# Where two of eight activation slots lie in SBUF: one slot shifted instead of two

## The chip, the core and the metric

The kernel runs on one core of a Trainium2 chip. The metric is the device time of one execution in microseconds; less is better. A profile of one execution gives the start and duration of every instruction on each engine. PE is TensorE's stream of matmuls, PEld its weight loads, DVE is VectorE, ACT is ScalarE, POOL is GpSimd, SP the queue that issues most DMAs.

## What is computed

The reference is one step of a two-layer diffusion trunk on 128 context tokens and 128 latent tokens of width 2048, all in fp32. Cut to what matters here:

```
for l in range(2):
    shift, scale, gate = adaLN(c) @ ada_w[l]
    h = rms_norm(x) * (1 + scale) + shift
    x = x + gate * mixer_l(h)            # attention | conv, or S5 | attention, with in and out projections
    h = rms_norm(x) * (1 + scale2) + shift2
    a = relu(h @ mlp_w1[l])              # 2048 -> 8192
    x = x + gate2 * ((a * a) @ mlp_w2[l])  # 8192 -> 2048
```

Nearly all the work is projections of a [256, K] activation by a large weight matrix. The two MLPs are the largest part.

## The kernel before

**Tiling.** Activations are kept transposed: a tile has 128 features on the partitions and the 256 tokens along the free axis. An output tile of 128 features is summed in one PSUM bank over all input tiles. `part` (L525) does eight input tiles (K = 1024) of one output tile; `linear` (L542) calls it twice. Most parts have eight blocks; a few have four.

**Split precision.** Weights and activations are both split into a high and a low fp32r half. A weight piece of 128x1024 arrives by DMA in `raw`, ACT writes its rounded half `wh`, DVE writes the rest `wl`. An activation tile becomes a slot of 512 elements: 256 of the high half, then 256 of the low half; ACT writes the first, DVE the second (`put`, L609). `block` (L518) is the inner step, three matmuls of 256 columns for one input tile: wh by the high half, wh by the low half, wl by the high half. Every matmul has a weight load of its own. The trace shows a block as two rows: `lin<-hl,wh` x2, then `lin<-hl,wl` x1. A block's length is the time from its `wh` row to the next block's `wh` row.

**Where activations lie.** The class `Arena` (L78) is one SBUF tile named `hl` with three groups. A group holds eight slots, for input tiles k with k % 8 = 0 to 7, so a part of eight blocks walks through the slots 0 to 7 of one group. In the built program the arena begins 384 bytes past a multiple of 512 and slots are 2048 bytes apart; all groups keep that remainder. So an unshifted slot lies at 384 past a multiple of 512 bytes, for the high and the low half alike. `SHIFT` adds elements of 4 bytes to the start of a slot. The weights `wh` and `wl` lie at 64 past a multiple of 512 throughout. Some activations, half or all of an MLP chunk's hidden tiles, lie in a pool of their own, also named `hl` in the trace: there all slots lie at 384, with no shift. Those for the not yet normalised input of an MLP or layer (`wide`, 258 columns) are packed differently and are not touched by `SHIFT`.

**Counts.** All projections come to 5632 blocks (16,896 matmuls). 304 of them are wide, 1152 read the pool, and the other 4176 read shiftable slots, 522 for each of the slots 0 to 7.

**Order.** A recorder plays all strands of the program against a cost table and writes down one fixed order for each engine. `part` lets other strands in between blocks before k = 2, 4 and 6 (`BREAKS`, L158): matmuls of attention, of S5, or of the adaLN projection (`ada`, L635) then stand between two blocks of a part.

Of the kernel before, what the change touches and what calls it, by code (L numbers as in the profile page):

```python
# [77 lines left out]
class Arena:  # L78
# [2 lines left out]

    SLOT, GROUP, WIDE, SHIFT = 512, 8 * 512 + 128, 516, (0, 0, 0, 0, 0, 0, 32, 40)

    def __init__(self, kern, pool):
        self.kern, self.n = kern, 0
# [1903 lines left out]
```

## Time and profile before

| | us |
|---|---|
| median of 3 runs (2397.22 to 2399.66) | 2398.15 |
| the profiled execution | 2397.81 |
| its span, first to last instruction | 2396.0 |
| PE busy | 2307.9 |
| DVE busy | 1695.7 |
| ACT busy | 1153.0 |

A matmul's row has its start and a modelled duration of about 0.28 us, of which the next matmuls overlap the larger part; what a matmul costs the stream is the distance from its start to the next start, about 0.113 us. So the distances between rows are to be read, not the durations. The rows give starts to 10 ns; a difference of a few ns shows when several blocks are added up.

### The profile page before, as it was taken

What the parts mean: (1) busy time and instruction counts of PE and PEld (TensorE: products, weight loads), DVE (VectorE), ACT (ScalarE), POOL (GpSimd) and SP (SyncE); (2) the same over time, 40 slices, a digit from 0 to 9 for tenths busy, and PEclk for the clock granted to TensorE, in tenths of its full rate; (3) what the DMA queues carried; (4) which work ended last, traced back from release to release, by engine and by line L of the source; (5) the groups of instructions that cost most, each with busy time, mean ns of one, the idle gap of its engine ahead of it and who ended that gap; (6) DMA issues with size and microseconds to landing.
All of it is one profiled execution on the core that took longest, in us unless ns stands there. A gap on an engine that the chain in (4) does not pass through costs nothing.

```text
span 2396.0 us, 49506 instructions
## 1 busy us (share of the span) xinstructions
PE 2307.9 (96%) x20152; PEld 2107.8 (88%) x20152; DVE 1695.7 (71%) x2957; ACT 1153.0 (48%) x1894; POOL 173.1 (7%) x293
## 2 busy tenths in 40 slices
PE   6999999999999999999999978899999999999997
PEld 1788887888999999999999757699999999999997
DVE  1489985677889898888767534566999855655565
ACT  1364457466444434434455744445744333543553
POOL 0000000000011011101000246000000000000000
PEclk9999999999999999999999988899999999999998
DMA  9979997879678889879877877766588855555552
GB/s 384 334 265 317 326 315 260 297 263 326 217 253 308 309 313 304 309 272 340 280 240 252 291 287 258 259 231 203 170 292 290 276 195 192 192 193 190 193 188 95
DMA packets 179637, 627.64 MB, mean 262 GB/s; under 512 B 21376, under 2 KB 21392, under 8 KB 179152
## 3 DMA queue, kind: packets, MB, share of 16 engines
q1 hardware_dynamic: 169920, 595.67, 71.6%
q0 software_dynamic: 9488, 28.81, 3.9%
q8 instruction: 158, 2.59, 0.4%
q14 instruction: 71, 0.58, 0.1%
HBM read 602.17 MB, written 26.41 MB: 262 GB/s over the span
## 4 chain that ended last, share of the span: by engine, by line
PE 85%; DMA 4%; DVE 4%; ACT 3%; POOL 3%; issue 1%; DVEq 0%; SPq 0%; ACTq 0%; POOLq 0%
PE lin L60 75%; PE ada L60 5%; POOL rt L60 2%; DMA raw<-in_ada_w 1%; DVE wl L60 1%; ACT wh L60 1%; DMA raw<-in_ew_in 1%; POOL hs L60 1%; DMA raw<-m3d 1%; PE m1T L60 1%; PE po L60 1%; ACT hs L60 0%; PE ps L60 0%; DVE hl L60 0%; DMA raw<-in_w 0%
## 5 line engine op out<-in xcount | busy, mean ns | idle before, releaser
L60 PE MATMUL lin<-hl,wh 128*128 128x256 f32 (+1 forms) x11200 | 1981.8, 281 | 5.5 <-ACT wh L60 5.0
L60 PEld LDWEIGHTS lin<-hl,wh 128*128 128x128 f32 x11200 | 1703.1, 189 | 97.4 <-issue 60.4
L60 PE MATMUL lin<-hl,wl 128*128 128x256 f32 (+1 forms) x5600 | 1559.4, 278 | 12.1 <-DVE wl L60 11.9
L60 PEld LDWEIGHTS lin<-hl,wl 128*128 128x128 f32 x5600 | 1055.6, 189 | 14.7 <-DVE wl L60 14.7
L60 DVE TENSOR_TENSOR wl<-raw,wh 128x1024 fp32r<-128x1024 f32 (+1 forms) x716 | 857.6, 1207 | 272.0 <-ACT wh L60 268.7
L60 ACT CAST wh<-raw 128x1024 fp32r<-128x1024 f32 (+1 forms) x716 | 738.6, 1036 | 507.6 <-PE lin L60 260.4
L60 PE MATMUL ada<-raw,condp 128*32 128x512 f32 (+1 forms) x1408 | 188.9, 574 | 20.1 <-DMA raw<-in_ada_w 19.9
L60 DVE SCALAR_TENSOR_TENSOR x<-lin,mod,x 128x128 f32<-128x128 f32 x320 | 97.1, 345 | 92.5 <-PE lin L60 92.4
L60 DVE SCALAR_TENSOR_TENSOR va<-raw,condp,va 128x1024 f32<-128x1024 f32 x120 | 148.4, 1278 | 0.0
L60 ACT ACTIVATE ms<-lin 128x256 f32<-128x256 f32 x114 | 43.6, 383 | 136.1 <-PE lin L60 136.0
L60 ACT CAST hl<-mq 128x256 fp32r<-128x256 f32 x128 | 51.9, 406 | 109.9 <-DVE mq L60 109.8
L60 PEld LDWEIGHTS ada<-raw,condp 128*32 128x32 f32 x1408 | 33.1, 109 | 74.9 <-DMA raw<-in_ada_w 34.1
L60 DVE SCALAR_TENSOR_TENSOR cv<-cin,pke,cv 128x256 f32<-128x256 f32 x232 | 96.6, 477 | 0.0
L60 ACT ACTIVATE sq<-x 128x256 f32<-128x256 f32 x75 | 31.0, 417 | 116.4 <-DVE x L60 114.5
L60 DVE SCALAR_TENSOR_TENSOR mq<-lin,ms 128x256 f32<-128x256 f32 x114 | 47.9, 421 | 53.3 <-ACT ms L60 53.2
L60 DVE TENSOR_TENSOR hl<-mq,hl 128x256 fp32r<-128x256 f32 x128 | 53.6, 421 | 27.4 <-ACT hl L60 27.4
L60 POOL TENSOR_TENSOR x<-x,rb 128x512 f32<-128x512 f32 (+1 forms) x2 | 4.2, 2130 | 906.0 <-ACT rb L60 906.0
L60 DVE TENSOR_TENSOR acc<-acc,sq 128x256 f32<-128x256 f32 x75 | 31.8, 423 | 32.3 <-ACT sq L60 30.5
L60 DVE TENSOR_TENSOR hl<-h,hl 128x256 fp32r<-128x256 f32 (+1 forms) x112 | 45.3, 419 | 9.1 <-ACT hl L60 8.7
L60 ACT CAST hl<-h 128x256 fp32r<-128x256 f32 (+1 forms) x112 | 42.7, 401 | 12.1 <-DVE h L60 11.4
L60 POOL DMA_DIRECT2D m3d<-m x32 | 21.5, 677 | 342.8 <-DVE m L60 341.6
L60 DVE TENSOR_TENSOR w<-s5z,bc 128x576 f32<-128x576 f32 x64 | 45.5, 752 | 0.6
(281 smaller groups left out, 1167.8 us busy)
## 6 DMA issues: line engine op xcount, KB each, us to landing
raw<-in_w SPq DMA_DIRECT2D x512, 512.0 KB, 5.1
raw<-in_ada_w SPq DMA_DIRECT2D x352, 512.0 KB, 6.2
raw<-in_ew_in SPq DMA_DIRECT2D x68, 512.0 KB, 6.1
raw<-in_ow_in SPq DMA_DIRECT2D x40, 512.0 KB, 6.2
raw<-in_ada_w SPq DMA_DIRECT2D x64, 256.0 KB, 6.2
raw<-in_ew_out SPq DMA_DIRECT2D x32, 512.0 KB, 5.9
raw<-in_ow_out SPq DMA_DIRECT2D x32, 512.0 KB, 4.5
m3d<-m POOLq DMA_DIRECT2D x32, 256.0 KB, 6.6
```

The costliest lines, as they stand in the source:

```text
L60: return f(out, *a, **kw)
```

## The change

`SHIFT` has one entry for each slot of a group. Before, slot 6 is moved by 32 elements (128 bytes, to 0 past a multiple of 512) and slot 7 by 40 (160 bytes, to 32 past). After, slot 6 is not moved (384 past) and slot 7 is moved by 32 (0 past).

```
-    SLOT, GROUP, WIDE, SHIFT = 512, 8 * 512 + 128, 516, (0, 0, 0, 0, 0, 0, 32, 40)
+    SLOT, GROUP, WIDE, SHIFT = 512, 8 * 512 + 128, 516, (0, 0, 0, 0, 0, 0, 0, 32)
```

Nothing else differs: the size of the arena is the same, every engine has the same instructions in the same order, and they wait for the same semaphores.

## Rows read from the trace of the kernel before

**Rows 1.** The page: parts 1 and 4, and two groups of part 5.
```profile
PE 2307.9 (96%) x20152; PEld 2107.8 (88%) x20152; DVE 1695.7 (71%) x2957; ACT 1153.0 (48%) x1894; POOL 173.1 (7%) x293
...
PE 85%; DMA 4%; DVE 4%; ACT 3%; POOL 3%; issue 1%; DVEq 0%; SPq 0%; ACTq 0%; POOLq 0%
...
L60 PE MATMUL lin<-hl,wh 128*128 128x256 f32 (+1 forms) x11200 | 1981.8, 281 | 5.5 <-ACT wh L60 5.0
...
L60 PE MATMUL lin<-hl,wl 128*128 128x256 f32 (+1 forms) x5600 | 1559.4, 278 | 12.1 <-DVE wl L60 11.9
```

**Rows 2.** Stages: length, busy us of PE, PEld, DVE, ACT, POOL; granted clock, DMA.
```profile
300.00:450.00 150.00, 145.17 (x1164) 119.44 (x1162) 101.10 (x218) 91.22 (x193) 5.94 (x11) 0.98 0.86 294
...
600.00:750.00 150.00, 150.00 (x1425) 145.44 (x1424) 133.30 (x232) 63.78 (x92) 22.05 (x35) 1.00 0.75 252
...
1350.00:1500.00 150.00, 122.64 (x1274) 99.96 (x1266) 59.71 (x108) 73.76 (x124) 77.69 (x134) 0.90 0.79 283
...
2100.00:2250.00 150.00, 150.00 (x1315) 150.00 (x1314) 85.94 (x110) 65.77 (x79) 0.00 (x0) 1.00 0.58 194
```

**Rows 3.** Timeline of PE near the end: start us, us, instruction.
```profile
2371.45 0.39 PE L60 MATMUL lin<-hl,wh 128*128 128x256 f32 x2
...
2373.49 0.40 PE L60 MATMUL lin<-hl,wh 128*128 128x256 f32 x2
...
2373.84 0.40 PE L60 MATMUL lin<-hl,wh 128*128 128x256 f32 x2
...
2374.20 0.39 PE L60 MATMUL lin<-hl,wh 128*128 128x256 f32 x2
...
2376.92 0.39 PE L60 MATMUL lin<-hl,wh 128*128 128x256 f32 x2
...
2378.96 0.40 PE L60 MATMUL lin<-hl,wh 128*128 128x256 f32 x2
...
2379.32 0.40 PE L60 MATMUL lin<-hl,wh 128*128 128x256 f32 x2
```

**Rows 4.** Timeline of PE, early in layer 0.
```profile
141.86 0.40 PE L60 MATMUL lin<-hl,wh 128*128 128x256 f32 x2
...
142.21 0.40 PE L60 MATMUL lin<-hl,wh 128*128 128x256 f32 x2
...
142.57 0.39 PE L60 MATMUL lin<-hl,wh 128*128 128x256 f32 x2
```

**Rows 5.** Timeline of PE around 900 us, from an adaLN fill on.
```profile
896.52 0.61 PE L60 MATMUL ada<-raw,condp 128*32 128x512 f32 x4
...
897.53 0.40 PE L60 MATMUL lin<-hl,wh 128*128 128x256 f32 x2
...
900.00 0.40 PE L60 MATMUL lin<-hl,wh 128*128 128x256 f32 x2
...
902.12 0.40 PE L60 MATMUL lin<-hl,wh 128*128 128x256 f32 x2
...
902.47 0.40 PE L60 MATMUL lin<-hl,wh 128*128 128x256 f32 x2
...
902.82 0.39 PE L60 MATMUL lin<-hl,wh 128*128 128x256 f32 x2
...
904.86 0.40 PE L60 MATMUL lin<-hl,wh 128*128 128x256 f32 x2
```

**Rows 6.** Timeline of PE around 1724 us, from a wait on.
```profile
1723.48 0.39 PE L60 MATMUL lin<-hl,wh 128*128 128x256 f32 x1 [0.51 <-DVE hl L60]
...
1723.83 0.40 PE L60 MATMUL lin<-hl,wh 128*128 128x256 f32 x2
...
1725.95 0.40 PE L60 MATMUL lin<-hl,wh 128*128 128x256 f32 x2
...
1726.66 0.39 PE L60 MATMUL lin<-hl,wh 128*128 128x256 f32 x2
```

**Rows 7.** Waits of PE from 450 to 1350 us: total, times, longest.
```profile
PE lin L60 <- DVE wl L60: 0.9, 1, 0.9
```

## The prediction

> **What bounds the kernel now.** I read the page first. PE is busy 96% of the span and holds 85% of the chain that ended last; its projection matmuls waited 5.5 and 12.1 us in all [rows 1]. The table of stages then says where that holds: between 600 and 750 us and between 2100 and 2250 us PE is busy for the whole stage, while between 300 and 450 us it is 145 of 150, and between 1350 and 1500 us (the S5 scan) 123 of 150 at a granted clock of 0.90 [rows 2]. From 450 to 1350 us PE's waits sum to 0.9 us [rows 7]. So in the MLPs a nanosecond saved per matmul reaches the end, and the change touches matmuls alone: it adds and removes no instruction. All depends on how long a block takes from a slot at 384, at 0 and at 32 past a multiple of 512.
>
> **A block at each address.** Near the end the timeline holds a whole part from shifted slots, then one from the pool, then the kernel's last shifted pair [rows 3]. The slots 0 to 5 run from 2371.45 to 2373.49: 2.04 us, 340 ns each. Slot 6 takes until 2373.84, slot 7 until 2374.20: 350 and 360 ns. The pool part that follows, all at 384, takes 2.72 us to 2376.92: eight times 340, its sixth and seventh as fast as the rest, so it is the address and not the place in the part that costs. Over all parts I measured the distances of starts: slot 6 takes 353.3 ns (353 blocks that follow a 340 ns block, the first at 141.86 us, the last at 2378.96 [rows 3 to 4]) and slot 7 takes 356.7 behind it. Call this the **short beat**.
>
> **A second beat.** Around 900 us the timeline shows a part behind an adaLN fill [rows 5]. It reads the pool and has seven blocks from 897.53 to 900.00: 353 ns each, from the same address 384. The next part, from shifted slots, stays so: 2.12 us from 900.00 to 902.12, 353 a block. Its slots 6 and 7 take 350 each, and from 902.82 on six blocks take 2.04 us again. So the same address has a **long beat** of 353 ns as well. It begins where foreign matmuls or a wait have interrupted the stream. It ends only behind the shifted pair: among 2909 blocks of 340 or 353 ns in the slots 0 to 5 and 1121 in the pool, none falls back from 353 to 340 inside a run at 384, while in all 96 cases in which nothing came between, the stream behind a pair entered in the long beat was in the short one. Of the 522 pairs 353 are entered in the short beat and 158 in the long one, the rest with an interruption just ahead. In the long beat slot 6 takes 349.4 and slot 7 353.9 ns on average, a little less than 384 would. The two shifted slots thus cost 30 ns for each part in the short beat, and they are what releases the stream from the long beat, worth 13.3 ns a block until the next interruption.
>
> **The change part by part.**
> - Slot 6 goes to 384, entered in the short beat: 353.3 becomes 340.0, 13.3 saved.
> - Slot 7 goes to 0 past, entered in the short beat: now it stands behind a 384 block as slot 6 did, so I take slot 6's 353.3 for 356.7, 3.4 saved. Together 16.7 ns by 353 parts: 5.9 us.
> - Entered in the long beat: slot 6 353.5 for 349.4 (4.1 lost), slot 7 349.4 for 353.9 (4.5 saved): nothing, over 158 parts.
> - The writes of the slots by ACT and DVE move with them: same size, and their order and waits stay. I count nothing; PE is the cover.
> - Of the 353 parts in the short beat 193 lie behind 1553 us, where PE is busy throughout bar a few waits: 3.2 us, all kept. 127 lie between 450 and 1350 us: 2.1 us, kept, with waits of 0.9 us there that could eat some. 33 lie where DMA, the convolution or the scan end waits: 0.55 us, of which I keep a third. Sum 5.4 us.
>
> The trace does not show one number: what three matmuls at 0, alone, leave behind. In the trace they are always followed by three at 32. If they release the stream like the pair, the sum stands. If not, the bound is the long beat kept all the way (below). I take the release, because the stream's first reaction to slot 6 is already different from the long beat (349.4 on average, some blocks down at 346), because both shifted addresses behave alike in cost (353.3 and 356.7), and because streams in the long beat come out of the pair in the short one whichever length slot 6 had.
>
> The page TensorE: Matmul & The Clock Gate of the Trainium skill (Part 2, step by step) says that PE has two independent SBUF read ports, so that loading the next weights takes no read bandwidth from the running matmul. By that rule no address matters and the sum is zero. The rows above disagree: 340, 353 and 357 ns for the same block at three addresses, and two beats at one address.
>
> **Forecast.** The profiled execution took 2397.81, its span 2396.0; what lies around the span is 1.8 and does not change. 2397.81 less 5.4 is 2392.4. The median lies 0.34 above the profiled execution, so the forecast for a median is 2398.15 less 5.4, 2392.8. What this kernel's measurement can tell from no change is about 0.2%, 4.8 us: the forecast lies just beyond it.
>
> **The rivals.**
> - *The release fails wholly.* One slot at 0 leaves a stream in its long beat; every stream then keeps that from its first interruption on. A part of 2750 ns (six by 340, 353.3, 356.7) becomes seven by 353.3 and 349.4: 2822, 72 more, by 353 parts 25.7 us; the 1038 pool blocks of 340 by 13.3 add 13.8. Of 39.5 us some 37 reach the end: 2435. It decides as soon as the long beat comes out of slot 7 unchanged. For it speaks one place [rows 6]. After a wait inside slot 7 two matmuls at 32 were left of the pair, and the stream went into the next part in the long beat, 2.12 us for six blocks from 1723.83 to 1725.95; the full pair then released it (340 again from 1726.66). So a short kick can be too little. Against it: three matmuls are more than two, and that stream had just been started anew.
> - *One slot at 0 throws the short beat out.* The shifted slot releases the long beat but ejects the short one, since nothing behind it sets it right. Then parts alternate: half of 25.7 and of 13.8, less 16.7 for the 177 short parts left (3.0): 16.8, some 15 at the end: 2413.
> - *The release fails at times.* The long beat enters slot 6 in several rhythms (346 to 353 ns). If one in three is not released, some 53 of 158 streams keep it for a part more, 72 to 106 ns each: 3.8 to 5.6 us, which gives the gain back: 2397 to 2398, and up to 2403 if failures follow each other.
> - *Nothing happens*, as by the rule above if the cost sat in the place and not in the address: 2398. The pool part that takes 2.72 us speaks against it [rows 3].
>
> **How the numbers follow.** Release works: 0.55, 2391 to 2395, the likeliest; of it I put 0.41 beyond 0.2% faster and 0.14 within. Fails at times: 0.15, of it 0.09 within and 0.06 slower. Alternation: 0.13, slower. Fails wholly: 0.14, slower. Nothing happens: 0.03, within. That gives faster 0.41, same 0.26, slower 0.33. The first, second and last case hold 0.73; to reach 0.8 the range goes up to the middle of the alternation, 2413. Below, if the waits of the early stages shrank too and all 5.9 us and a little more were kept, 2391.
>
> **What would show it.** In the changed kernel's timeline of PE near the end, a part of shifted slots should take 2.73 us instead of 2.75: seven blocks of 340 and one of 353. Behind an adaLN fill the part in the long beat should again be followed by one in the short beat. If instead six blocks at 384 take 2.12 us behind an uninterrupted slot 7, the release has failed; if that is so in every second part late in the last MLP, where no fill stands, it is the alternation. If DVE's waits for `wh` or PE's for `wl` grow by some us, the gain went there. The prediction is wrong if slot 7 at 0 takes other than about 353 ns in the short beat, or if the number of parts in the long beat changes.

## The result and the profile after

| | before | after |
|---|---|---|
| median of four runs, us | 2397.68 (2395.14 to 2399.66) | 2432.44 (2429.24 to 2435.01) |
| the profiled execution, its span | 2397.81, 2396.0 | 2435.01, 2433.2 |
| PE busy | 2307.9 | 2344.2 |

Before has one run more than the three ahead of the prediction, so its median is 0.5 lower. The ratio is 1.0145, 95% interval 1.0133 to 1.0156. The change costs 34.8 us where 5.4 had been forecast as a gain; the time lies above the range (2391 to 2413). The rival *The release fails wholly* had given 2435.

The page of after, the lines that answer to [rows 1]:

```profile
PE 2344.2 (96%) x20152; PEld 2144.1 (88%) x20152; DVE 1698.7 (70%) x2957; ACT 1152.0 (47%) x1894; POOL 172.9 (7%) x293
...
PE 84%; DMA 4%; DVE 4%; ACT 4%; POOL 3%; issue 1%; DVEq 0%; SPq 0%; ACTq 0%; POOLq 0%
...
L60 PE MATMUL lin<-hl,wh 128*128 128x256 f32 (+1 forms) x11200 | 2019.1, 282 | 5.4 <-ACT wh L60 5.1
...
L60 PE MATMUL lin<-hl,wl 128*128 128x256 f32 (+1 forms) x5600 | 1569.0, 280 | 11.5 <-DVE wl L60 11.4
```

PE is busy 36.3 us longer with the same 20,152 matmuls. The waits ahead of the projections stay (5.5 and 12.1 us before, 5.4 and 11.5 now), the other engines are busy as long as before to 3 us, and the shares of the chain are the same to 1%. So no wait was added: the matmuls themselves take longer. The two stages in which PE never stops say the same (columns as in [rows 2]):

```profile
600.00:750.00 150.00, 150.00 (x1396) 145.42 (x1396) 129.29 (x227) 63.21 (x91) 20.74 (x33) 1.00 0.73 242
...
2100.00:2250.00 150.00, 150.00 (x1276) 150.00 (x1275) 83.06 (x107) 63.02 (x75) 0.00 (x0) 1.00 0.57 189
```

1396 matmuls where there were 1425, 1276 where there were 1315, at the same granted clock of 1.00. Between 450 and 1350 us PE waits even less than in [rows 7]:

```profile
PE lin L60 <- DVE wl L60: 0.2, 1, 0.2
```

The timeline of PE near the end, against [rows 3]: a part from the arena and the pool part behind it, at the starts of slot 0, slot 6, slot 7, the pool part and the next part.

```profile
2408.93 0.40 PE L60 MATMUL lin<-hl,wh 128*128 128x256 f32 x2
...
2411.05 0.40 PE L60 MATMUL lin<-hl,wh 128*128 128x256 f32 x2
...
2411.40 0.40 PE L60 MATMUL lin<-hl,wh 128*128 128x256 f32 x2
...
2411.75 0.40 PE L60 MATMUL lin<-hl,wh 128*128 128x256 f32 x2
...
2414.58 0.40 PE L60 MATMUL lin<-hl,wh 128*128 128x256 f32 x2
```

The slots 0 to 5 take 2.12 us where they took 2.04, the pool part 2.83 where it took 2.72: every block at 384 takes 353 ns. No fill and no wait stands near; this is the long beat, kept. It is so in every part from 2330 us to the end. Summed over all blocks of 256 columns, from a block's start to the next matmul of any kind (uninterrupted are those of up to 362 ns; the others stand apart), the two executions differ by:

| us | before | after | difference |
|---|---|---|---|
| slots 0 to 5 | 1000.0 | 1026.7 | +26.7 |
| pool, all at 384 | 382.5 | 396.3 | +13.8 |
| slot 6 | 177.5 | 177.7 | +0.3 |
| slot 7 | 144.1 | 141.7 | -2.4 |
| interrupted blocks | 203.3 | 202.7 | -0.6 |

Sum 37.7, of a span 37.2 longer. Of the blocks at 384 in the slots 0 to 5, 2150 were short and 759 long before; now those in the slots 0 to 6 are 151 short and 3261 long. In the pool 1038 short and 83 long became 8 and 1113.

### The profile page after: what moved, and what is told of

Read it like the earlier page. It is cut to its first block, busy times and chain, and to the rows that moved or that the text cites. A ratio compares the mean times of both kernels' runs of the same rounds, so it can differ in the third digit from the quotient of the medians.

```text
span 2433.2 us, 49506 instructions
## 1 busy us (share of the span) xinstructions
PE 2344.2 (96%) x20152; PEld 2144.1 (88%) x20152; DVE 1698.7 (70%) x2957; ACT 1152.0 (47%) x1894; POOL 172.9 (7%) x293
## 4 chain that ended last, share of the span: by engine, by line
PE 84%; DMA 4%; DVE 4%; ACT 4%; POOL 3%; issue 1%; DVEq 0%; SPq 0%; ACTq 0%; POOLq 0%
PE lin L60 74%; PE ada L60 5%; POOL rt L60 2%; DVE wl L60 1%; DMA raw<-in_ew_in 1%; DMA raw<-in_ada_w 1%; ACT wh L60 1%; POOL hs L60 1%; PE m1T L60 1%; DMA raw<-m3d 1%; ACT hs L60 0%; PE ps L60 0%; PE sc L60 0%; PE po L60 0%; DMA raw<-in_w 0%
## 5 line engine op out<-in xcount | busy, mean ns | idle before, releaser
L60 PE MATMUL lin<-hl,wh 128*128 128x256 f32 (+1 forms) x11200 | 2019.1, 282 | 5.4 <-ACT wh L60 5.1
L60 PE MATMUL lin<-hl,wl 128*128 128x256 f32 (+1 forms) x5600 | 1569.0, 280 | 11.5 <-DVE wl L60 11.4
```

The source lines that it names most:

```text
L60: return f(out, *a, **kw)
```

## The experiments

For each kernel I counted, over the whole trace, in which beat a stream enters the shifted slots and in which it leaves them, where nothing interrupts it (up to 347 ns a block short, up to 362 long). On the chips of these runs the kernel before took 2398.55 beside e1 to e4, 2396.35 beside e5 and e6, and 2398.09 beside e7 to e9. All but e6 and e7 ran once; single runs of one kernel differ by some us (the four of after by 5.8), so the argument rests on the counts, and single times less than 6 us apart are not told from each other. The edits are shown against the kernel before, where nothing else is said; the line of `SHIFT` is shortened to that name, and `...` stands for lines that are left out.

| kernel | bytes past a multiple of 512, in the order read | entered long, leaves short | entered short, leaves short | us |
|---|---|---|---|---|
| before | 0, 32 | 92 of 93 | 288 of 288 | 2397.68 |
| after | 384, 0 | 0 of 370 | 0 of 13 | 2432.44 |
| e1_last32 | 384, 32 | 0 of 372 | 10 of 10 | 2431.61 |
| e2_both0 | 0, 0 | 0 of 364 | 0 of 17 | 2436.62 |
| e3_none | 384, 384 | none seen | stays short | 2434.43 |
| e4_both32 | 32, 32 | 1 of 378 | 0 of 4 | 2437.20 |
| e6_early | 0, 32 at tiles 2, 3 | 131 of 131 | 342 of 342 | 2393.82 |
| e7_fewer | the same, fewer groups | 131 of 131 | 254 of 254 | 2392.02 |
| e8_reversed | 32, 0 at tiles 2, 3 | 0 of 460 | 0 of 14 | 2437.37 |
| e9_apart | 0, 384, 32 at tiles 2, 3, 4 | 0 of 477 behind the 0, 0 of 483 behind the 32 | 0 of 12 behind the 0 | 2434.53 |

That the long beat is kept was plain from the trace of after. Open was what in the old pair had released it: the slot at 32, the length of the kick (six matmuls off 384 where now there are three), or the sequence; and whether the slot at 0 does harm of its own.

**One slot, at 32** (e1_last32).

```
-    SHIFT = (0, 0, 0, 0, 0, 0, 32, 40)
+    SHIFT = (0, 0, 0, 0, 0, 0, 0, 40)
```

> Only half of the change: slot 6 goes to 384, slot 7 stays at 32 past a multiple of 512. Theory A (the address of the last slot decides: 32 releases the long beat, 0 does not): every stream behind an uninterrupted slot 7 has 340 ns a block, slot 6 costs 340 for 353, 4.7 us less than before, about 2393. Theory B (the number of shifted matmuls decides: six release, three do not) and theory C (the step from 0 to 32 between the two slots releases): 353 ns a block nearly throughout, as in the changed kernel, about 2432.

Measured: 2431.61, nothing released in 372 cases. A slot at 32 alone does not do it. But it does not throw a stream out of the short beat either. The timeline of PE: slots 1, 7 of one part, slots 0 and 6 of the next:

```profile
183.34 0.39 PE L60 MATMUL lin<-hl,wh 128*128 128x256 f32 x2
...
185.38 0.40 PE L60 MATMUL lin<-hl,wh 128*128 128x256 f32 x2
...
185.74 0.39 PE L60 MATMUL lin<-hl,wh 128*128 128x256 f32 x2
...
187.78 0.39 PE L60 MATMUL lin<-hl,wh 128*128 128x256 f32 x2
```

Six blocks in 2.04 us, the slot at 32 in 0.36, and again six in 2.04: a stream in the short beat goes through. The slot itself takes 354.2 ns here, behind a block at 384; the 356.7 of before are the price of 32 behind 0. In after the same place in a part ends it. Its timeline, from an adaLN fill on: slots 1 and 7, then slots 0 and 3 of the next part.

```profile
212.69 0.61 PE L60 MATMUL ada<-raw,condp 128*32 128x512 f32 x4
...
213.68 0.39 PE L60 MATMUL lin<-hl,wh 128*128 128x256 f32 x2
...
215.72 0.40 PE L60 MATMUL lin<-hl,wh 128*128 128x256 f32 x2
...
216.07 0.40 PE L60 MATMUL lin<-hl,wh 128*128 128x256 f32 x2
...
217.14 0.40 PE L60 MATMUL lin<-hl,wh 128*128 128x256 f32 x2
```

Six blocks in 2.04 us behind the fill, so this stream started in the short beat; slot 7 at 0 takes 0.35; the next three blocks take 1.07, over 353 each. So the single slot at 0 throws the short beat out (13 of 13 cases) and does not release the long one.

**Both slots at 0** (e2_both0), the length of the kick without the 32.

```
+    SHIFT = (0, 0, 0, 0, 0, 0, 32, 32)
```

> The other half of the change: slot 6 stays at 0, slot 7 goes from 32 to 0 past a multiple of 512. Theory A (the last slot's address decides): no release, about 2432. Theory B (six shifted matmuls release): released, slot 7 takes 353 for 357, about 2396. Theory C (the step from 0 to 32 releases): no release, about 2432.

Measured: 2436.62, 0 of 364 released, 17 of 17 short streams ejected. In the timeline, slots 1, 6 and 7 of a part, then slots 0 and 6 of the next: five blocks in 1.71 us, the two at 0 in 0.35 each, then six in 2.12.

```profile
246.97 0.39 PE L60 MATMUL lin<-hl,wh 128*128 128x256 f32 x2
...
248.68 0.40 PE L60 MATMUL lin<-hl,wh 128*128 128x256 f32 x2
...
249.03 0.40 PE L60 MATMUL lin<-hl,wh 128*128 128x256 f32 x2
...
249.38 0.40 PE L60 MATMUL lin<-hl,wh 128*128 128x256 f32 x2
...
251.50 0.40 PE L60 MATMUL lin<-hl,wh 128*128 128x256 f32 x2
```

**Both slots at 32** (e4_both32).

```
+    SHIFT = (0, 0, 0, 0, 0, 0, 40, 40)
```

> Both slots at 32 past a multiple of 512. Theory A (the last slot's address decides) and theory B (six shifted matmuls): released, slot 6 takes 357 for 353, about 2399. Theory C (the step from 0 to 32): no release, 353 ns a block nearly throughout, about 2434.

Measured: 2437.20, 1 of 378 released. Six matmuls off 384 are not enough at either address, so the length of the kick is not the cause.

**No shift** (e3_none).

```
+    SHIFT = (0, 0, 0, 0, 0, 0, 0, 0)
```

> No slot is shifted. If a shifted slot is the only thing that changes the beat at all, streams keep the beat with which they start after an interruption: about as the changed kernel, 2430 to 2434, with a few more parts of 340 ns since nothing ejects them. If instead the single slot at 0 is what throws streams into the long beat of 353 ns, the short beat comes back and the time is about 2392.

Measured: 2434.43. No stream goes from long to short by itself; all blocks near the end take 353 ns. Two starts of PE, eight blocks apart, 2.82 us:

```profile
2299.87 0.40 PE L60 MATMUL lin<-hl,wh 128*128 128x256 f32 x2
...
2302.69 0.40 PE L60 MATMUL lin<-hl,wh 128*128 128x256 f32 x2
```

And a stream that starts short stays short until it is interrupted. So the time of after (2432.44) is not told from that of a kernel without any shift: its one slot earns nothing that the runs show.

**Other pairs** (e5_scan). 15 of the uses of a group get another pair; the remaining ones keep 0, 32.

```
...
+            self.last_two[part] = self.TRY.get((part, self.seen[part]), (32, 40))
...
-        a = self.groups[part] * self.GROUP + j * width + (0 if wide else self.SHIFT[j])
+        a = self.groups[part] * self.GROUP + j * width + (0 if wide or j < 6 else self.last_two[part][j - 6])
```

> Each group of slots gets a pair of its own (bytes past a multiple of 512 of the slots 6 and 7), to see in one trace which pairs release the long beat: in layer 0 384/416, 480/0, 384/448 and 384/64 in the mixer, 416/448 and 384/480 for the MLP's input, 384/128, 448/480, 384/256 and 0/64 for its hidden tiles; in layer 1's MLP 384/0 and 0/128 for the input, 480/32, 0/16 and 0/48 for the hidden tiles. Theory C1 (a step of 32 bytes up between the two shifted slots releases): 480/0, 416/448 and 448/480 release all streams, the others none. Theory C2 (it takes the way over 0 to 32): none of these releases, and 353 ns a block lasts from the first interruption to the end wherever no pair 0/32 is left, about 2430. Theory D (some single address other than 0 and 32 releases): at least one of 384/416, 384/448, 384/480, 384/64, 384/128 does.

Measured: 2429.01 where before took 2396.35. Not one of 323 streams entered long is released by the 15 other pairs: 384 then 416 (8 cases), 480 then 0 (18), 384 then 448 (8), 384 then 64 (9), 416 then 448 (38), 384 then 480 (38), 384 then 128 (13), 448 then 480 (10), 384 then 256 (12), 0 then 64 (11), 384 then 0 (57), 0 then 128 (55), 480 then 32 (15), 0 then 16 (16), 0 then 48 (15). In the same execution the groups left at 0 then 32 release 10 of 10. So a step of 32 bytes is not enough (416 then 448, 480 then 0), nor a start at 0 with some other second address (16, 48, 64, 128). Three of the single addresses tried behind 384 also eject the short beat: 480 (6 of 6), 416 and 256 (one case each); 128 does not (3 of 3 stay short).

One thing more lies in this trace. The text counts addresses by their remainder to 512, but a remainder to 256 fits as well: 128 past behaves as 384 does, and 256 past as 0. In the long beat a slot at 128 takes 353.5 ns (13 cases; 353.4 at 384) and a slot at 256 takes 349.1 (12 cases; 348.9 at 0); in the short beat they take 340 and 353. Slots 6 and 7 and the next block, with slot 7 at 128; then the same three with slot 7 at 256, and the seventh block of the next part:

```profile
643.48 0.39 PE L60 MATMUL lin<-hl,wh 128*128 128x256 f32 x2
...
643.82 0.39 PE L60 MATMUL lin<-hl,wh 128*128 128x256 f32 x2
...
644.16 0.39 PE L60 MATMUL lin<-hl,wh 128*128 128x256 f32 x2
...
1084.31 0.39 PE L60 MATMUL lin<-hl,wh 128*128 128x256 f32 x2
...
1084.65 0.40 PE L60 MATMUL lin<-hl,wh 128*128 128x256 f32 x2
...
1085.01 0.40 PE L60 MATMUL lin<-hl,wh 128*128 128x256 f32 x2
...
1087.13 0.40 PE L60 MATMUL lin<-hl,wh 128*128 128x256 f32 x2
```

The slot at 128 takes 0.34 us like the one before it. The slot at 256 takes 0.36, and the six blocks behind it 2.12. No run tried a pair such as 256 then 288, so which period holds is not shown.

**The pair earlier in the part** (e6_early). The input tiles 2 and 3 lie in the two shifted slots, the others move up.

```
+        j = j if wide else (0, 1, 6, 7, 2, 3, 4, 5)[j]
```

> The pair at 0 and 32 is kept, but the input tiles 2 and 3 of each part lie in the shifted slots instead of 6 and 7 (tiles 4 to 7 move into the slots 2 to 5). If the pair releases wherever it stands and a restart in front of it is no hindrance, streams that are interrupted ahead of a part keep the long beat for two blocks instead of six: 53 ns less for some 120 parts, 6.5 us, and those interrupted before their blocks 4 and 6 keep it longer, 2 to 4 us: about 2395. If the release depends on where in the part the pair stands (on the weights' columns or on the breaks before blocks 2 and 4), the streams stay at 353 ns, about 2432.

Measured: 2393.82 in ten runs against 2396.35, ratio 0.9987 (0.9977 to 0.9996). The pair releases there too, 131 of 131. The timeline of PE: tiles 0, 2, 3, 4, then the starts of the next two parts.

```profile
1909.12 0.40 PE L60 MATMUL lin<-hl,wh 128*128 128x256 f32 x2
...
1909.83 0.40 PE L60 MATMUL lin<-hl,wh 128*128 128x256 f32 x2
...
1910.18 0.40 PE L60 MATMUL lin<-hl,wh 128*128 128x256 f32 x2
...
1910.54 0.39 PE L60 MATMUL lin<-hl,wh 128*128 128x256 f32 x2
...
1911.90 0.39 PE L60 MATMUL lin<-hl,wh 128*128 128x256 f32 x2
...
1914.62 0.39 PE L60 MATMUL lin<-hl,wh 128*128 128x256 f32 x2
```

Two blocks in 0.71 us, the pair in 0.71, then four in 1.36 and the pool's eight in 2.72. A stream that a part starts in the long beat loses two blocks instead of six: 289 long blocks in the arena where there were 759.

**The order of the two** (e8_reversed, its edit shown against e6_early): tile 2 at 32, tile 3 at 0.

```
-        j = j if wide else (0, 1, 6, 7, 2, 3, 4, 5)[j]
+        j = j if wide else (0, 1, 7, 6, 2, 3, 4, 5)[j]
```

> The pair stands at input tiles 2 and 3 as in e6_early, but tile 2 lies at 32 past a multiple of 512 and tile 3 at 0. If it is the order 0 then 32 that releases a stream from the long beat, nothing releases here: streams entering in the long beat leave it in the long beat (0 of about 370 released), and the time is near 2435, as with no shift or one. If the pair releases as a pair, in either order, about 130 of 130 are released and the time is 2394. A third outcome, a pair that ejects the short beat as the single slot at 0 does, would show as streams entering short and leaving long.

Measured: 2437.37, 0 of 460 released, 14 of 14 short streams ejected. In the timeline, tiles 1, 2, 3, 4 and 7: one block in 0.34 us, the pair in 0.70, three blocks in 1.06.

```profile
167.37 0.39 PE L60 MATMUL lin<-hl,wh 128*128 128x256 f32 x2
...
167.71 0.40 PE L60 MATMUL lin<-hl,wh 128*128 128x256 f32 x2
...
168.06 0.40 PE L60 MATMUL lin<-hl,wh 128*128 128x256 f32 x2
...
168.41 0.40 PE L60 MATMUL lin<-hl,wh 128*128 128x256 f32 x2
...
169.47 0.40 PE L60 MATMUL lin<-hl,wh 128*128 128x256 f32 x2
```

**The two apart** (e9_apart, its edit shown against e6_early): tile 2 at 0, tile 3 at 384, tile 4 at 32.

```
-        j = j if wide else (0, 1, 6, 7, 2, 3, 4, 5)[j]
+        j = j if wide else (0, 1, 6, 2, 7, 3, 4, 5)[j]
```

> Tile 2 lies at 0, tile 3 at 384 and tile 4 at 32: the same two addresses in the same order, with one ordinary block between them. If the step straight from 0 to 32 releases, nothing is released: 2434 to 2438. If it is enough that three matmuls at 0 come some time ahead of three at 32, streams come out short, and the time is near 2394. In the short beat the block between should tell too: the single slot at 0 alone ejected the short beat, so by the first view tile 3 stands in the long beat.

Measured: 2434.53, nothing released behind either slot, and the short beat thrown out by the 0 in 12 of 12 cases. The step must go straight from 0 to 32, and in this order.

**Fewer pairs** (e7_fewer, its edit shown against e6_early), e6_early without the pair where nothing interrupts any more.

```
+    PLAIN = (("h1", 4), ("hid", 6), ("hid", 7))
...                                       # self.seen counts the uses of a group
-        a = self.groups[part] * self.GROUP + j * width + (0 if wide else self.SHIFT[j])
+        a = self.groups[part] * self.GROUP + j * width + (0 if wide or (part, self.seen[part]) in self.PLAIN else self.SHIFT[j])
```

> e6_early without the pair in three uses of a group in the second MLP: the second half of its input (h1) and the hidden tiles of its last two chunks. In e6_early nothing interrupts the stream behind 1910 us but a wait at the end, and a stream in the short beat stays there without any shift, so there a pair only costs: 353.4 + 356.5 - 680 = 30 ns, on some 85 parts 2.5 us. Expected 2391.3 where e6_early took 2393.8, a ratio to the kernel before of 0.998. If the short beat needs the pair to last, some hundred parts fall into the long beat and the time grows by up to 6 us, to 2400.

Measured: 2392.02 in nine runs against 2398.09, ratio 0.9975 (0.9965 to 0.9985). 89 parts lost their pair, and the short beat lasts without it. One of them, from its first block to the next part, eight blocks in 2.72 us:

```profile
2300.45 0.39 PE L60 MATMUL lin<-hl,wh 128*128 128x256 f32 x2
...
2303.17 0.39 PE L60 MATMUL lin<-hl,wh 128*128 128x256 f32 x2
```

89 times 30 ns are 2.7 us. The ratios of e6_early and e7_fewer, from different chips, have intervals that overlap, so the gain of the one over the other is likely, not shown; that e7_fewer beats the kernel before, by 6 us, is.

## Why the prediction was wrong

- **The step that failed** is "I take the release". The prediction had said that the trace of before does not show what three matmuls at 0, alone, leave behind, and filled the gap by three reasons. None of them bore on it. What the runs showed in its place: behind one slot at 0, 0 of 370 streams were released and 13 of 13 short ones were thrown out. That slot 6 already took 349.4 ns in the long beat told nothing of what comes behind: in after slot 7 at 0 takes 349.7, and the stream is long again behind it. That both addresses cost alike (353.3 and 356.7) told nothing of what they do to the stream: 0 ejects, 32 holds, and only 0 followed by 32 releases. That the pair released whichever length slot 6 had was true of the pair alone.
- **The price of an address** was right. Slot 7 at 0, entered short, takes 353.9 ns (353.3 forecast), entered long 349.7 (349.4). But with 15 uninterrupted short entries left (353 before) there was nothing to save it on.
- **The two beats and their worth** were right: 340 and 353 ns, the long one kept until a release. The rival *The release fails wholly* took 39.5 us from them, some 37 of it at the end. Measured are 34.8 between the medians and 37.2 between the two spans; by the table above slots 0 to 7 gave 24.5 (25.7 in the working) and the pool 13.8 (13.8).
- **[rows 6]** could not decide. The prediction read them as a kick that was too short. But slot 6 at 0 and the first matmul of slot 7 had run ahead of the wait:

```profile
1722.34 0.40 PE L60 MATMUL lin<-hl,wh 128*128 128x256 f32 x2
...
1722.70 0.28 PE L60 MATMUL lin<-hl,wh 128*128 128x256 f32 x1
```

  Behind the wait stood two matmuls at 32 and no 0. By e1_last32 and e4_both32 three or six at 32 do not release either. And most streams are long behind an interruption, whatever stands there (185 of 192, below). So the place spoke for the failure no more than other restarts did. A rival that had spelt out "the pair releases as a sequence" would have had the same time, 2435.
- **The alternation** was half right: one slot at 0 does eject the short beat. It needs a release as well, which there is not, so no part in two is short; near the end all are long. And the ejection decides little: e1_last32, whose slot at 32 ejects nothing, takes 2431.61 in its one run; nearly all streams start in the long beat anyway (in before the first whole block behind an interrupted one is long in 185 of 192 cases).
- **Nothing happens** was wrong as expected. The Trainium skill (TensorE: Matmul & The Clock Gate, Part 2, step by step) has a weight load take no read bandwidth from the running matmul. The prediction took from it that no address matters. The runs here move by 1.45% on addresses alone, and the measurement decides; whether a weight load takes part in it no run shows.
- **Small slips** in the working change nothing: the kept terms (3.2, 2.1 and a third of 0.55) come to 5.5 and not 5.4; behind a pair entered long, with nothing in between, 92 of 93 streams are short and not all of 96; and 8 of the 158 long entries have an interruption just ahead.
- **The chances**: the whole failure had 0.14, so the range could stop at 2413 and leave it out. The far end of the unseen number had been worked out nearly right; what was wrong was how little weight it got beside reasons that no row bore out.

What the runs settle is the rule, that 0 directly followed by 32 releases and nothing else tried does. They don't settle why: which resource has to be met in which order. Nor do they tell why a stream behind an interruption takes one beat or the other. They do show that the first block behind other matmuls already tells which. Counted over all eleven traces, where that block takes less than 480 ns, it took 427, 428 or 448 to 450 ns in 153 of 157 streams that then ran short, and in 2 of 1750 that ran long (those took 435 to 447 or 455 to 469). The block at 213.23 us ahead of the short stream in after took 449, the one at 897.07 us ahead of the long stream of [rows 5] took 463. This speaks for a matter of timing at the start, but no run set that timing.

## What to carry to other kernels

Where a kernel holds an odd constant that works as a pair, and the trace shows the effect of the pair alone, half of it is an unknown and not half the effect: take both ends into the range. Where the same instruction has two lasting lengths in one trace, count transitions, what each stretch enters with and leaves with, ahead of averages: the value of the shift lay in what it did to some 3000 blocks behind it and not in the 30 ns of its own. Such a release is best put early in a stretch, and only where something interrupts (e7_fewer, ratio 0.9975).

## What the runs showed of the hardware

- A stream of 128x256 fp32r matmuls, each with its own weight load, runs in one of two lasting rhythms at the same granted clock of 1.00: 340 ns for three (113.3 a matmul) or 353 (117.7), over hundreds of blocks and without a wait.
- Which one depends on history. In the kernels here the start addresses of the moving operand, taken modulo 512, change it (modulo 256 would fit the runs as well): 0, then 32 directly behind it, turns long into short (354 of 355 cases in before, e6_early and e7_fewer); 0 alone, twice, or behind 32 turns short into long (56 of 56 in after, e2_both0, e8_reversed and e9_apart), 32 alone changes neither beat (10 of 10 short ones stay, 0 of 372 long ones end), 32 twice turns short into long (4 of 4).
- The price of one block in the short beat is 340.0 ns at 384, 353 at 0 and 354 at 32 behind a block at 384, and 357 at 32 behind 0. The lasting effect on the blocks behind, 13.3 ns each, is what decided the time here.
